# A masked scan for the log decays, and another order of 32x32 products, in a hybrid state-space and DeltaNet layer on Trainium2

## The chip, the cores and the metric

The kernel runs on one core of one Trainium2 chip. The metric is the device time of one execution in microseconds (us), as the median of several runs. A core has five engines that run side by side, each through its own list of instructions in order: TensorE (PE in the profile, with its weight loads as PEld), VectorE (DVE), ScalarE (ACT), GpSimd (POOL) and SyncE (SP), which here issues nearly all DMA transfers. They wait for each other by semaphores.

## The reference

One layer over a sequence of 1024 frames with 2048 channels: an RMSNorm, one input projection, an S5 state-space branch and a gated DeltaNet branch, gates, an output projection and a final RMSNorm. The change is in the DeltaNet branch (8 heads of 128), of which this is the part that matters:

```python
beta = jax.nn.sigmoid(beta_logit)
g = -jnp.exp(_f32(a_log)) * jax.nn.softplus(a_logit + _f32(dt_bias))   # log decay, per frame and head
...
gc = jnp.cumsum(g, axis=-1)                                            # within a chunk
decay = jnp.exp(jnp.where(causal, gc[..., :, None] - gc[..., None, :], -jnp.inf))
kk = jnp.einsum("bhncd,bhnsd->bhncs", k, k)
a_mat = jnp.where(strict, beta[..., None] * kk * decay, 0.0)
sol = lax.linalg.triangular_solve(a_mat, rhs, left_side=True, lower=True, unit_diagonal=True)
...
qk = jnp.einsum("bhncd,bhnsd->bhncs", q, k) * decay
```

So each chunk needs the matrix exp(gc[t] - gc[s]) for s <= t, which is exp of the sum of g over the frames after s up to t, and the inverse of a unit triangular matrix.

## The kernel before, in words

The kernel goes over the sequence in two passes of 512 frames. In each pass the heads are worked on in four chunks of 128 frames. The bulk of the work is projections on TensorE: each fp32 weight is split into a high and a low part in the fp32r type (`whi` by ACT, `wlo` by DVE, in `w_prep`), and each product is three matmuls of 128x512 (high by high, high by low, low by high). In the profile these are `p<-X,whi`, `p<-X,wlo`, `p<-Y,whi` and so on; this text calls them large matmuls.

All other work is written as generators in lanes (`epi`, `io`, `chain`, `prep`, `tab`, `s5`, `out`, `x`). After each group of three large matmuls `pump` calls `step` for every lane, and a lane's next piece is put into the program at that place if a small model of the engines' clocks (`Clock`, with the costs in `COST`) says that what it waits for is done and that DVE is not too far ahead of PE. So the order of all engines' instructions is fixed when the program is written, by the model's costs. The model charges an fp32 matmul of at most 32 output rows 0.3 of max(n/600, 0.06) us, whatever part of the array it uses, and a scan on DVE 0.07 + 0.00128 n us.

The pieces that the change touches:

- `gates_prep`, once in each pass, computes `gt` (g of every frame, for 8 heads x 4 chunks), splits it into `gth` and `gtl`, and makes the sums that are needed per frame with three small matmuls against `causal`, `after_r` and `ones`.
- `d_prep(h)`, once for each head and pass (16 times), in the lane `prep`. It first makes the log decays: POOL multiplies one part of g (`gth` or `gtl`) for two chunks with the mask `causal` into `dhl`, and PE multiplies `after_r` (1 where the frame is later) with it, four matmuls of 256 columns into one PSUM bank `pD`. ACT takes the exponential into the tile `E`, and POOL masks it. Then come the products of keys and queries (`pA`), and the inverse: 16x16 diagonal blocks on POOL (through DRAM, `lu_d` and `tu_d`), then joined to 32, 64 and 128 on PE. `Tm` is the same memory as `E`.
- The join to 32 and 64 is four bursts of 32x32 products, with operands in the tile that the profile calls M. First burst: `pG` from `LU` and `Tm`, 16 products, for each diagonal part b of the array (rows and columns 32b to 32b+31) and each chunk c. Second: `pU`, 32 products, from `g3` and `U`. Third: `pG`, 8 products, on two parts (rows 0 or 64, columns 32 or 96). Fourth: `pU`, 16 products, on four parts (rows 32 and 96, two column parts each). Every product is fp32 and shows in the trace as two matmuls, each with its weight load. After each burst ACT or DVE takes the bank out of PSUM.
- `d_chain(h)` in the lane `chain` runs the recurrence over chunks with the results.

A profile row has the line of the helper that records operations (L135) for nearly all work; tiles tell the groups apart. M is the one big block in which `E`, `LU`, `U`, `mi` and the heads' operands lie.

Of the kernel before, what the change touches and what calls it, by code (L numbers as in the profile page):

```python
# [11 lines left out]
F32 = mybir.dt.float32  # L12
F32R = mybir.dt.float32r
I32 = mybir.dt.int32
AF = mybir.ActivationFunctionType
# [21 lines left out]
P = 128  # L37
# [110 lines left out]
def kernel(  # L148
# [27 lines left out]
    V = Timed(nc.vector, "V", clock)  # L176
    S = Timed(nc.scalar, "S", clock)
    G = Timed(nc.gpsimd, "G", clock)
    PE = Timed(nc.tensor, "PE", clock)
    SP = Timed(nc.sync, "Q", clock)  # L180
# [3 lines left out]
    cpool = ctx.enter_context(tc.tile_pool(name="cpool", bufs=1))  # L184
# [4 lines left out]
    dram = ctx.enter_context(tc.tile_pool(name="dram", bufs=1, space=bass.MemoryType.DRAM))  # L189
# [4 lines left out]
    def nm(s):  # L194
        uid[0] += 1
        return f"{s}_{uid[0]}"

    def bank(i):
        return psum.tile([P, 512], F32, tag=f"p{i}", name=nm(f"p{i}"))
# [7 lines left out]
    def small(tag, n, rows=P):  # L207
        if tag not in small_at:
            small_at[tag] = small_at.get("", 0)
            small_at[""] = small_at[tag] + n  # L210
        return smalls[0:rows, small_at[tag]:small_at[tag] + n]

    def tt(o, a, b, op, eng=None):
        (eng or V).tensor_tensor(o, a, b, op=op)
# [10 lines left out]
    MUL, ADD, SUB, MAX, MIN = ALU.mult, ALU.add, ALU.subtract, ALU.max, ALU.min  # L225


    ident = cpool.tile([P, P], F32, name="ident")
    make_identity(nc, ident)
    ones = cpool.tile([P, P], F32, name="ones")  # L230
    G.memset(ones, 1.0)
    causal = cpool.tile([P, P], F32, name="causal")
# [3 lines left out]
    after = tmp[:, 0:P]  # L236
# [5 lines left out]
    for b in range(4):  # L242
# [2 lines left out]
        G.memset(off16[s32, 0, :], -1.0)  # L245
        G.affine_select(off16[s32, 0, :], off16[s32, 0, :], pattern=[[0, 16]], compare_op=ALU.is_ge,
                        fill=0.0, base=-16, channel_multiplier=1)
    after_r = cpool.tile([P, P], F32R, name="after_r")
    S.activation(after_r, after, AF.Copy)
    halfpi = cpool.tile([P, 1], F32, name="halfpi")  # L250
    G.memset(halfpi, float(np.float32(math.pi / 2)))

# [23 lines left out]

    lu_d = [dram.tile([4, 129, P], F32, name=f"lu_d{i}") for i in range(2)]
    tu_d = [[dram.tile([4, 129, P], F32, name=f"tu_d{i}{j}") for j in range(2)] for i in range(2)]
    nq_d = [dram.tile([1, P, 16], F32, name=f"nq_d{i}") for i in range(2)]
    st_d = dram.tile([8, P, P], F32, name="st_d")  # L280
    td_d = dram.tile([16, P, T], F32, name="td_d")
# [2 lines left out]
    def part(d, off, *dims):  # L284

        a = d[:, :, :] if len(d.shape) == 3 else d[:, :, :, :]
        return bass.AP(tensor=a.tensor, offset=a.offset + off, ap=[list(x) for x in dims])
# [46 lines left out]
    def exp_pool(o, v, n):  # L334
        G.tensor_tensor(o, pexp["e"][:, 0:1].broadcast_to([P, n]), v, op=ALU.pow)

    def gts(o, a, s1, s2, op0, op1):
        G.tensor_scalar(o, a, s1, s2, op0=op0, op1=op1)
# [10 lines left out]
    for ps_ in range(NPASS):  # L349
# [8 lines left out]
        for c in range(8):  # L358
            if c % 2 == 0 and 8 - u0 + c // 2 < 8:
                i = 8 - u0 + c // 2  # L360
# [503 lines left out]
    def hold(cond):  # L864
        while not cond():
            yield -1
# [147 lines left out]


    gt = cpool.tile([P, 8, 4], F32, name="gt")
    gth = cpool.tile([P, 8, 4], F32, name="gth")
    gtl = cpool.tile([P, 8, 4], F32, name="gtl")
    bt = cpool.tile([P, 8, 4], F32, name="bt")
    ex = cpool.tile([P, 3, 32], F32, name="ex")  # L1020
    negc = cpool.tile([P, 32], F32, name="negc")
# [1 line left out]
    def gates_prep(lg, ps_):  # L1023

        yield from hold(lambda: (ps_, "M0") in done)
        yield max(clock.wr[c] for c in clock.cells(lg))
        p2 = bank(5)
        fold = small("fold", 16, 32)
        tt(fold, ident[0:32, 0:16], ident[0:32, 16:32], ADD)
        for t in range(4):  # L1030
            PE.matmul(p2[:, t * 16:(t + 1) * 16], lhsT=lg[:, t * P:(t + 1) * P], rhs=fold, start=True, stop=True)
        l3 = p2[:, 0:64].rearrange("p (t h) -> p h t", h=16)
        mif = dw["mi"].rearrange("p c n -> p (c n)")
        av = mif[:, 0:32]
        a3 = av.rearrange("p (h t) -> p h t", h=8)
        S.activation(bt, l3[:, 0:8, :], AF.Tanh, scale=0.5)
        tt(a3, l3[:, 8:16, :], dtb.unsqueeze(2).broadcast_to([P, 8, 4]), ADD)
        gts(bt, bt, 0.5, 0.5, MUL, ADD)
        if ps_ == 0:
            exp_pool(nega, nega, 8)  # L1040
            gts(nega, nega, -1.0, 0.0, MUL, ADD)

        na, e1, w1, y0, e2, dl = (mif[:, (i + 1) * 32:(i + 2) * 32] for i in range(6))
        stt(na, av, -1.0, av, MUL, MIN)
        exp_pool(e1, na, 32)
        gts(w1, e1, 1.0, 1.0, MUL, ADD)
        S.activation(y0, w1, AF.Ln)
        yield
        gts(dl, w1, -1.0, 1.0, MUL, ADD)
        tt(dl, e1, dl, ADD, eng=G)  # L1050
        gts(na, y0, -1.0, 0.0, MUL, ADD)
        exp_pool(e2, na, 32)
        tt(dl, dl, e2, MUL, eng=G)
        tt(e2, w1, e2, MUL, eng=G)
        gts(e2, e2, 1.0, -1.0, MUL, ADD)
        tt(y0, e2, y0, ADD, eng=G)
        tt(y0, y0, dl, ADD, eng=G)
        gts(av, av, 0.0, 3e38, MAX, MIN)
        tt(y0, y0, av, ADD, eng=G)
        tt(gt, y0.rearrange("p (h t) -> p h t", h=8), nega.unsqueeze(2).broadcast_to([P, 8, 4]), MUL, eng=G)  # L1060
        yield
        gf = gt.rearrange("p h t -> p (h t)")
        S.activation(gth.bitcast(F32R), gt, AF.Copy)
        tt(gtl, gt, gth, SUB, eng=G)
        p3 = bank(5)
        for i, m in enumerate((causal, after_r.bitcast(F32), ones)):
            PE.matmul(p3[:, i * 32:(i + 1) * 32], lhsT=m, rhs=gf, start=True, stop=True)
        exf = ex.rearrange("p a n -> p (a n)")
        ts(exf, p3[:, 0:96], -1000.0, None, MAX)
        exp_pool(exf, exf, 96)  # L1070
        gts(negc, ex[:, 0, :], -1.0, 0.0, MUL, ADD)
        yield -1

    dhl = cpool.tile([P, 2, P], F32R, name="dhl")
    nk = [small(f"nk{i}", 4) for i in range(2)]
    nq = [small(f"nq{i}", 4) for i in range(2)]
    cc = [small(f"cc{i}", 4) for i in range(2)]
# [13 lines left out]
    def d_prep(h, ps_):  # L1091
        st = dw["set"][h % 2]
        kq, v, qk, U, kd = st["kq"], st["v"], st["qk"], st["U"], st["kd"]
        E, LU, mi = dw["E"], dw["LU"], dw["mi"]
        nk_, nq_, cc_ = nk[h % 2], nq[h % 2], cc[h % 2]
        qs_ = small(f"qs{h % 2}", 16)
        lud, tud = lu_d[h % 2], tu_d[h % 2]
        pD = bank(5)
        for j in range(2):
            for i, gg in enumerate((gth, gtl)):  # L1100
                tt(dhl, gg[:, h, 2 * j:2 * j + 2].unsqueeze(2).broadcast_to([P, 2, P]),
                   causal[:, None, :].broadcast_to([P, 2, P]), MUL, eng=G)
                yield
                PE.matmul(pD[:, j * 256:(j + 1) * 256], lhsT=after_r, rhs=dhl.rearrange("p c n -> p (c n)"),
                          start=(i == 0), stop=(i == 1))
        S.activation(E.rearrange("p c n -> p (c n)"), pD, AF.Exp)
        tt(E, E, hb4(causal), MUL, eng=G)
        yield -1
        yield from until((ps_, "q", h))
# [21 lines left out]
        for hf in range(2):  # L1131
            pA = bank((5, 2)[hf])
            for c in (2 * hf, 2 * hf + 1):
                PE.matmul(pA[:, (c % 2) * 256:(c % 2) * 256 + 256], lhsT=kq[:, c, 0, :],
                          rhs=kq[:, c].rearrange("p a n -> p (a n)"), start=True, stop=True)
# [10 lines left out]
        SP.dma_start(rows(lud), LU)  # L1146
        yield
        mif = mi.rearrange("p c n -> p (c n)")
        Ef = E.rearrange("p c n -> p (c n)")
        ba = mif[0:32, 0:256].rearrange("p (i m) -> p i m", i=16)  # L1150
        btm = mif[0:32, 256:512].rearrange("p (i m) -> p i m", i=16)
        bx = Ef[0:32, 0:256].rearrange("p (i m) -> p i m", i=16)
# [6 lines left out]
        for j in range(15):  # L1159
            n = 15 - j  # L1160
            a = ba[:, j, j + 1:16].unsqueeze(2).broadcast_to([32, n, j + 1])
            b = btm[:, j:j + 1, 0:j + 1].broadcast_to([32, n, j + 1])
# [22 lines left out]
        gs = mi  # L1185
        g3 = mi[:, :, 0:32]
        B4 = [slice(32 * b, 32 * b + 32) for b in range(4)]
        for b in B4:
            for c in range(4):
                PE.matmul(pG[b, c * 32:(c + 1) * 32], lhsT=LU[b, c, b], rhs=Tm[b, c, b], start=True, stop=True)  # L1190
        tt(g3, pG[:, 0:P].rearrange("p (c n) -> p c n", c=4),
           off16.rearrange("p a c -> p (a c)")[:, None, :].broadcast_to([P, 4, 32]), MUL)
        tt(g3, g3, id32[:, None, :].broadcast_to([P, 4, 32]), ADD)
        yield
        pU = bank(2)
        for b in B4:
            for c in range(4):
                PE.matmul(pU[b, c * 32:(c + 1) * 32], lhsT=g3[b, c, :], rhs=U[b, c, b], start=True, stop=True)
                PE.matmul(pU[b, P + c * 32:P + (c + 1) * 32], lhsT=U[b, c, b], rhs=g3[b, c, :],
                          start=True, stop=True)  # L1200
        for b in B4:
# [4 lines left out]

        pG = bank(5)
        pg = pG.rearrange("p (c n) -> p c n", c=4)
        for o in (0, 64):
            for c in range(4):  # L1210
                PE.matmul(pg[o + 32:o + 64, c, 0:32], lhsT=LU[o:o + 32, c, o + 32:o + 64],
                          rhs=Tm[o:o + 32, c, o:o + 32], start=True, stop=True)
        for o in (0, 64):
# [1 line left out]
        yield  # L1215
        pU = bank(2)
        pu = pU.rearrange("p (c n) -> p c n", c=4)
        for o in (0, 64):
            for c in range(4):
                PE.matmul(pu[o:o + 32, c, 0:32], lhsT=gs[o + 32:o + 64, c, 0:32],  # L1220
                          rhs=U[o + 32:o + 64, c, o + 32:o + 64], start=True, stop=True)
                PE.matmul(pu[o + 32:o + 64, c, 0:32], lhsT=U[o + 32:o + 64, c, o + 32:o + 64],
                          rhs=gs[o + 32:o + 64, c, 0:32], start=True, stop=True)
        for o in (0, 64):
# [9 lines left out]
        for c in range(4):  # L1234
            PE.matmul(pg[64:128, c, 0:64], lhsT=LU[0:64, c, 64:128], rhs=Tm[0:64, c, 0:64],
                      start=True, stop=True)
# [4 lines left out]
        for c in range(4):  # L1241
            PE.matmul(pu[0:64, c, 0:64], lhsT=gs[64:128, c, 0:64], rhs=U[64:128, c, 64:128],
                      start=True, stop=True)
# [448 lines left out]
```

## Time and profile before

| | before |
|---|---|
| median of 3 runs | 2998.33 us (2996.68 to 3001.13) |
| the profiled execution's own time | 3000.75 us |
| its span, first to last instruction | 2998.7 us |
| granted TensorE clock | 0.996 of full speed |
| PE busy | 2952.0 us (98%) in 15902 matmuls |
| DVE busy | 1676.4 us (56%) |
| ACT busy | 1149.5 us (38%) |
| POOL busy | 460.2 us (15%) |
| DMA, mean | 135 GB/s |

A group of instructions has the form: line, engine, operation, output tile <- input tiles, shape, count | busy time, mean ns of one | idle time of the engine just before them, and what ended it. In the order of time a row has its start, its duration, and how many like instructions it merges. A stretch of time (a window) shows how long an engine was busy in it and, behind x, how many of its instructions overlap the stretch. Matmuls are pipelined, so their durations overlap; the step from one start to the next is what one of them takes of PE's time.

### The profile page before, as it was taken

To read this page: it belongs to the slowest core of one execution; us is meant where nothing else is said; L and a number is where in the kernel's file an instruction comes from. 1 tells how busy PE (TensorE), PEld (TensorE's weight loads), DVE (VectorE), ACT (ScalarE), POOL (GpSimd) and SP (SyncE) were. 2 spreads that over 40 slices of the span, in tenths; PEclk is the share of its full clock that TensorE was granted. 3 is DMA by queue.
4 is the path that set the end of the run, shared out by engine and by line. 5 is a ranking of instruction groups with operands and counts; after the bars stand their busy time and mean duration, and the time that the engine had idled before them with its cause. 6 is when DMAs were issued, how large, how long until landed. Compare 5 with 4: busy or idle time off the path is not lost.

```text
span 2998.7 us, 42470 instructions
## 1 busy us (share of the span) xinstructions
PE 2952.0 (98%) x15902; PEld 2372.9 (79%) x15902; DVE 1676.4 (56%) x3130; ACT 1149.5 (38%) x2483; POOL 460.2 (15%) x857
## 2 busy tenths in 40 slices
PE   8999999999999999999999999999999999999998
PEld 6877777777777888888878777777777788888887
DVE  5746777777767422553454676567556633226542
ACT  5434544554544222334333344333433322223331
POOL 4413222122200000000024221222122000000000
PEclk9999999999999999999999999999999999999999
DMA  6435445444545644446354444544444464445541
GB/s 166 125 79 145 115 131 135 112 123 122 135 136 161 195 119 119 145 137 239 120 162 133 116 116 117 137 120 115 123 127 122 137 198 123 118 125 155 195 149 57
DMA packets 618240, 405.29 MB, mean 135 GB/s; under 512 B 91257, under 2 KB 551218, under 8 KB 616114
## 3 DMA queue, kind: packets, MB, share of 16 engines
q1 hardware_dynamic: 615730, 394.19, 46.2%
q0 software_dynamic: 2304, 8.39, 0.8%
q8 instruction: 125, 2.05, 0.3%
q14 instruction: 81, 0.66, 0.1%
HBM read 335.79 MB, written 66.72 MB: 134 GB/s over the span
## 4 chain that ended last, share of the span: by engine, by line
PE 85%; DVE 6%; ACT 3%; POOL 2%; DMA 2%; issue 2%; SPq 1%; DVEq 0%; POOLq 0%; ACTq 0%
PE p L135 85%; DVE G0a L135 2%; DVE M L135 2%; POOL M L135 2%; DVE wlo L135 1%; ACT M L135 1%; DVE tmp L135 1%; SPq L135 1%; POOL smalls L135 1%; DMA M<-tu_d 0%; ACT tmp L135 0%; ACT whi L135 0%; ACT L135 0%; ACT G0b L135 0%; DMA raw<-in_w_in_dram 0%
## 5 line engine op out<-in xcount | busy, mean ns | idle before, releaser
L135 PE MATMUL p<-X,whi 128*128 128x512 f32 (+1 forms) x4432 | 1396.4, 397 | 1.5 <-DVE whi L135 0.8
L135 DVE TENSOR_TENSOR wlo<-raw,whi 128x512 fp32r<-128x512 f32 x920 | 633.2, 700 | 744.2 <-ACT whi L135 743.5
L135 PEld LDWEIGHTS p<-X,whi 128*128 128x128 f32 (+1 forms) x4432 | 802.0, 188 | 175.3 <-issue 17.9
L135 PE MATMUL p<-X,wlo 128*128 128x512 f32 (+1 forms) x2184 | 852.7, 390 | 0.3 <-DVE wlo L135 0.2
L135 ACT ACTIVATE whi<-raw 128x512 fp32r<-128x512 f32 x917 | 557.8, 625 | 519.0 <-PE p L135 487.2
L135 PE MATMUL p<-Y,whi 128*128 128x512 f32 (+1 forms) x1808 | 568.0, 396 | 0.9 <-ACT p L135 0.9
L135 PEld LDWEIGHTS p<-X,wlo 128*128 128x128 f32 x2184 | 410.9, 188 | 89.1 <-DVE wlo L135 0.9
L135 PEld LDWEIGHTS p<-Y,whi 128*128 128x128 f32 (+1 forms) x1808 | 330.7, 187 | 71.3 <-issue 3.9
L135 PE MATMUL p<-Y,wlo 128*128 128x512 f32 x896 | 349.7, 390 | 0.0
L135 POOL TENSOR_SCALAR smalls<-smalls 128x4 f32<-128x4 f32 (+1 forms) x58 | 18.2, 313 | 1584.8 <-DVE smalls L135 1116.3
L135 ACT ACTIVATE tmp<-p 128x512 f32<-128x512 f32 x160 | 95.5, 597 | 400.9 <-PE p L135 393.6
L135 POOL TENSOR_TENSOR M<-M 32x28 f32<-32x28 f32 (+8 forms) x492 | 196.7, 400 | 282.8 <-DMA M<-lu_d 200.1
L135 DVE TENSOR_TENSOR G0a<-G0a 128x256 f32<-128x256 f32 (+1 forms) x432 | 211.1, 525 | 7.2 <-ACT G0a L135 3.5
L135 PEld LDWEIGHTS p<-M 32*32 32x32 f32 (+2 forms) x3072 | 153.0, 123 | 72.6 <-ACT M L135 28.8
L135 PEld LDWEIGHTS p<-Y,wlo 128*128 128x128 f32 x896 | 168.1, 188 | 36.5 <-DVE wlo L135 0.4
L135 PE MATMUL p<-M 32*32 32x32 f32 (+3 forms) x3072 | 186.9, 215 | 6.9 <-DMA M<-tu_d 3.8
L135 ACT ACTIVATE M<-p 32x128 f32<-32x128 f32 (+3 forms) x337 | 98.9, 297 | 161.1 <-PE p L135 157.5
L135 DVE SCALAR_TENSOR_TENSOR tmp<-tmp,vec 128x512 f32<-128x512 f32 x144 | 112.0, 778 | 11.7 <-ACT tmp L135 8.3
L135 DVE TENSOR_TENSOR G0a<-p,G0a 128x512 f32<-128x512 f32 x128 | 82.0, 681 | 13.9 <-PE p L135 13.8
L135 DVE TENSOR_TENSOR_SCAN G0a<-rho,scar,G0a 128x256 f32<-128x256 f32 x128 | 89.3, 738 | 0.0
L135 PE MATMUL p<-whi,G0a 128*128 128x512 f32 x280 | 88.5, 391 | 0.0
L135 PE MATMUL p<-whi,X 128*128 128x512 f32 x256 | 82.2, 393 | 0.0
(209 smaller groups left out, 2640.7 us busy)
## 6 DMA issues: line engine op xcount, KB each, us to landing
raw<-in_w_in_dram SPq DMA_DIRECT2D x324, 512.0 KB, 4.0
raw<-in_w_out_dram SPq DMA_DIRECT2D x56, 512.0 KB, 4.0
raw<-in_dn_w_up_dram SPq DMA_DIRECT2D x32, 512.0 KB, 4.1
raw<-in_s_w_up_dram SPq DMA_DIRECT2D x32, 512.0 KB, 3.9
td_d<-tmp SPq DMA_DIRECT2D x32, 256.0 KB, 2.0
M<-tu_d SPq DMA_DIRECT2D x32, 256.0 KB, 3.2
cs_d<-G0a SPq DMA_DIRECT2D x32, 256.0 KB, 2.2
yg_d<-G0a SPq DMA_DIRECT2D x64, 128.0 KB, 2.4
```

The lines of the kernel that those rows point to most:

```text
L135: return f(*a, **k)
```

## The change

The log decays come from a scan. `gates_prep` also transposes g on PE to one row per head and chunk (`grow`, 32 x 128) and stores it in DRAM (`g_d`). `d_prep` loads the head's four rows into `E` on all 128 partitions, and DVE scans each chunk with state = (g + state) * strict, where strict is 1 for frames later than the partition's own. After the scan the value is the sum of g over the frames after s up to t. The exponential and the mask are as before. `gth`, `gtl`, `dhl` and their matmuls go, and `afterk` stands in for `after_r` with the same content.

In the four bursts the loop over chunks becomes the outer one and the loop over parts the inner one; in the second and the fourth the two kinds of product are also taken apart, so that a kind is done for all parts before the other begins (in the fourth, within a chunk).

```diff
-    after_r = cpool.tile([P, P], F32R, name="after_r")
-    S.activation(after_r, after, AF.Copy)
+    afterk = cpool.tile([P, P], F32, name="afterk")
+    S.activation(afterk, after, AF.Copy)
+    strict = cpool.tile([P, P], F32, name="strict")
+    tt(strict, causal, ident, SUB, eng=G)
...
+    g_d = dram.tile([1, 32, P], F32, name="g_d")
...
         gf = gt.rearrange("p h t -> p (h t)")
-        S.activation(gth.bitcast(F32R), gt, AF.Copy)
-        tt(gtl, gt, gth, SUB, eng=G)
         p3 = bank(5)
-        for i, m in enumerate((causal, after_r.bitcast(F32), ones)):
+        PE.transpose(p3[0:32, 96:96 + P], gf, ident)
+        for i, m in enumerate((causal, afterk, ones)):
             PE.matmul(p3[:, i * 32:(i + 1) * 32], lhsT=m, rhs=gf, start=True, stop=True)
+        grow = mif[0:32, 256:256 + P]
+        S.activation(grow, p3[0:32, 96:96 + P], AF.Copy)
+        SP.dma_start(g_d[0], grow)
...
-        pD = bank(5)
-        for j in range(2):
-            for i, gg in enumerate((gth, gtl)):
-                tt(dhl, gg[:, h, 2 * j:2 * j + 2].unsqueeze(2).broadcast_to([P, 2, P]),
-                   causal[:, None, :].broadcast_to([P, 2, P]), MUL, eng=G)
-                yield
-                PE.matmul(pD[:, j * 256:(j + 1) * 256], lhsT=after_r, rhs=dhl.rearrange("p c n -> p (c n)"),
-                          start=(i == 0), stop=(i == 1))
-        S.activation(E.rearrange("p c n -> p (c n)"), pD, AF.Exp)
+        Ef = E.rearrange("p c n -> p (c n)")
+        SP.dma_start(Ef, part(g_d, h * 512, (0, P), (1, 512)))
+        yield
+
+        for c in range(4):
+            V.tensor_tensor_scan(E[:, c, :], E[:, c, :], strict, 0.0, op0=ADD, op1=MUL)
+        S.activation(Ef, Ef, AF.Exp)
         tt(E, E, hb4(causal), MUL, eng=G)
...
-        for b in B4:
-            for c in range(4):
+        for c in range(4):
+            for b in B4:
                 PE.matmul(pG[b, c * 32:(c + 1) * 32], lhsT=LU[b, c, b], rhs=Tm[b, c, b], start=True, stop=True)
...
-        for b in B4:
-            for c in range(4):
+        for c in range(4):
+            for b in B4:
                 PE.matmul(pU[b, c * 32:(c + 1) * 32], lhsT=g3[b, c, :], rhs=U[b, c, b], start=True, stop=True)
+        for c in range(4):
+            for b in B4:
                 PE.matmul(pU[b, P + c * 32:P + (c + 1) * 32], lhsT=U[b, c, b], rhs=g3[b, c, :],
                           start=True, stop=True)
...
-        for o in (0, 64):
-            for c in range(4):
+        for c in range(4):
+            for o in (0, 64):
                 PE.matmul(pg[o + 32:o + 64, c, 0:32], lhsT=LU[o:o + 32, c, o + 32:o + 64],
                           rhs=Tm[o:o + 32, c, o:o + 32], start=True, stop=True)
...
-        for o in (0, 64):
-            for c in range(4):
+        for c in range(4):
+            for o in (0, 64):
                 PE.matmul(pu[o:o + 32, c, 0:32], lhsT=gs[o + 32:o + 64, c, 0:32],
                           rhs=U[o + 32:o + 64, c, o + 32:o + 64], start=True, stop=True)
+            for o in (0, 64):
                 PE.matmul(pu[o + 32:o + 64, c, 0:32], lhsT=U[o + 32:o + 64, c, o + 32:o + 64],
                           rhs=gs[o + 32:o + 64, c, 0:32], start=True, stop=True)
```

Three places show how the program's order changes. The first is PE at the start of `d_prep` for the last head of the second pass, before the change; X and Y are the large matmuls' operands, `ident,M` is the transpose in the chain of the head before.

```order
L135 MATMUL p_2443_19235<-dhl,after_r 128x256
L135 MATMUL p_2440_19207<-Y_1453_11621,whi_19130 128x512 x2
L135 MATMUL p_2440_19207<-Y_1453_11621,wlo_19131 128x512
L135 MATMUL p_2440_19207<-X_1454_11622,whi_19169 128x512 x2
L135 MATMUL p_2440_19207<-X_1454_11622,wlo_19170 128x512
L135 MATMUL p_2443_19235<-dhl,after_r 128x256
L135 MATMUL p_2440_19207<-X_1454_11622,whi_19169 128x512 x2
L135 MATMUL p_2440_19207<-X_1454_11622,wlo_19170 128x512
L135 MATMUL p_2449_19277<-ident,M_1692_13095 128x128 x4
```

And after the change, around the same transpose:

```order
L135 MATMUL p_2437_19247<-X_1446_11591,whi_19228 128x512 x2
L135 MATMUL p_2437_19247<-X_1446_11591,wlo_19229 128x512
L135 MATMUL p_2445_19311<-ident,M_1684_13064 128x128 x4
L135 MATMUL p_2437_19247<-X_1446_11591,whi_19228 128x512 x2
L135 MATMUL p_2437_19247<-X_1446_11591,wlo_19229 128x512
```

The matmuls with `dhl` are gone from between the large matmuls, and nothing stands in their place on PE.

The second place is DVE at the start of that head's `d_prep`, after the change. M with `strict` are the scans (printed as a scalar-tensor-tensor form), `wlo` the weight splits, `tmp` the convolution, G0a the S5 branch.

```order
L135 SCALAR_TENSOR_TENSOR tmp<-tmp,vec 128x512 x3
L135 TENSOR_TENSOR X_1828_14211<-M_1684_13064,X_1828_14211 128x512
L135 SCALAR_TENSOR_TENSOR M_1684_13064<-M_1684_13064,strict 128x128 x4
L135 TENSOR_TENSOR wlo_19192<-raw_19050,whi_19191 128x512
L135 TENSOR_TENSOR wlo_19209<-raw_19050,whi_19208 128x512
L135 SCALAR_TENSOR_TENSOR G0a_12911<-rho,scar,G0a_12911 128x256 x2
```

The four scans stand in DVE's list ahead of two weight splits; before the change DVE had no work for the log decays.

The third place is SP there, after the change: `M<-g_d` is the load of the head's rows, `raw` the weights.

```order
L135 DMA G0a_12911<-w_d 128x256
L135 DMA raw_19117<-in_w_in_dram 128x8x128
L135 DMA M_1684_13064<-g_d 128x512
L135 DMA raw_19189<-in_w_in_dram 128x8x128
L135 DMA raw_19226<-in_w_in_dram 128x8x128
```

The load stands between two weight loads, where before there were weight loads alone.

More of the change, by code (lines that the diff above doesn't have):

```diff
@@ L1016 @@
     gt = cpool.tile([P, 8, 4], F32, name="gt")
-    gth = cpool.tile([P, 8, 4], F32, name="gth")
-    gtl = cpool.tile([P, 8, 4], F32, name="gtl")
     bt = cpool.tile([P, 8, 4], F32, name="bt")
@@ L1072, in gates_prep @@
         yield -1
-    dhl = cpool.tile([P, 2, P], F32R, name="dhl")
     nk = [small(f"nk{i}", 4) for i in range(2)]
@@ L1148, in d_prep @@
         mif = mi.rearrange("p c n -> p (c n)")
-        Ef = E.rearrange("p c n -> p (c n)")
         ba = mif[0:32, 0:256].rearrange("p (i m) -> p i m", i=16)
```

## The prediction

> **What bounds the kernel now.** I read the page's first part and its chain of waits first.
>
> ```profile
> span 2998.7 us, 42470 instructions
> PE 2952.0 (98%) x15902; PEld 2372.9 (79%) x15902; DVE 1676.4 (56%) x3130; ACT 1149.5 (38%) x2483; POOL 460.2 (15%) x857
> PE 85%; DVE 6%; ACT 3%; POOL 2%; DMA 2%; issue 2%; SPq 1%; DVEq 0%; POOLq 0%; ACTq 0%
> ```
>
> TensorE (PE) is busy for 98% of the span and holds 85% of the chain that ended last. So time taken off PE comes off the end nearly in full, and work on DVE, ACT or POOL costs only where PE then waits for it. Next I read the groups of instructions, with each shape apart, for what the change touches.
>
> ```profile
> L135 PE MATMUL p<-M 32*32 32x32 f32 x2304 | 64.1, 193 | 4.1 <-DMA M<-tu_d 3.8 <-ACT M L135 0.2
> L135 PE MATMUL p<-dhl,after_r 128*128 128x256 f32 x64 | 20.6, 322 | 1.6 <-POOL dhl L135 1.6
> L135 PEld LDWEIGHTS p<-dhl,after_r 128*128 128x128 f32 x64 | 12.1, 188 | 7.8 <-POOL dhl L135 6.2
> L135 DVE TENSOR_TENSOR_SCAN G0a<-rho,scar,G0a 128x256 f32<-128x256 f32 x128 | 89.3, 738 | 0.0
> ```
>
> The 2304 small products are 144 for each of 16 heads (8 in each of two passes over the sequence): every fp32 product shows as two matmuls, so the four bursts of a head have 32, 64, 16 and 32. Busy times are unions of overlapping durations and don't give a price. For that I read the order of time on PE, in a head of the second pass (start, duration, what, count).
>
> ```profile
> 1908.90 0.39 PE L135 MATMUL p<-Y,wlo 128*128 128x512 f32 x1
> 1909.22 0.89 PE L135 MATMUL p<-M 32*32 32x32 f32 x32
> 1910.04 0.73 PE L135 MATMUL p<-Y,whi 128*128 128x512 f32 x2
> ...
> 1911.62 1.91 PE L135 MATMUL p<-M 32*32 32x32 f32 x64
> 1913.46 0.73 PE L135 MATMUL p<-Y,whi 128*128 128x512 f32 x2
> ...
> 1915.72 0.59 PE L135 MATMUL p<-M 32*32 32x32 f32 x16
> 1916.24 0.73 PE L135 MATMUL p<-Y,whi 128*128 128x512 f32 x2
> ...
> 1917.83 0.60 PE L135 MATMUL p<-M 32*32 32x32 f32 x32
> 1918.36 0.73 PE L135 MATMUL p<-X,whi 128*128 128x512 f32 x2
> ```
>
> A burst ends with a fixed gap. The second one covers 1911.62 to 1913.53, its last matmul lasts about 0.19 (mean 193 ns), so that one started at 1913.34, and the next large matmul starts at 1913.46: 0.12 later. The same 0.12 taken from each burst leaves 0.70, 1.72, 0.40 and 0.41 us in which matmuls are started: 22, 27, 25 and 13 ns for each. The fourth burst is twice as fast as the others, and it alone already changes between two parts of the array.
>
> How many run at once tells why. The same head, PE alone, work on M alone, in stretches of 0.01 us; x is the number of matmuls in flight.
>
> ```profile
> core 0: us, PE busy (x), PEclk, DMA share, GB/s
> 1912.00:1912.01 0.01, 0.01 (x6) 1.00 0.68 205
> 1918.00:1918.01 0.01, 0.01 (x13) 1.00 0.00 0
> 1918.07:1918.08 0.01, 0.01 (x19) 1.00 0.00 0
> 1918.15:1918.16 0.01, 0.01 (x18) 1.00 0.00 0
> ```
>
> At 1912.00, inside one diagonal part's run, 6 are in flight: 193/6 = 32 ns from one to the next. At 1918.00 the fourth burst has its first two parts going (13), and from 1918.07 the last products of those and the first of the next two run together: 18 or 19, that is 193/18.5 = 10 ns. So one part takes a matmul every 32 ns, and parts run beside each other, four of them at once here.
>
> **The change, part by part.** (1) Order of the products. In the first and second burst neighbours now go round four diagonal parts; in the third they alternate between two parts; in the fourth they go round four. At 10 ns with four parts and 193/13 = 15 ns with two, a head's bursts need 32 x 10 = 0.32, 64 x 10 = 0.64, 16 x 15 = 0.24 and 32 x 10 = 0.32 us, 1.52 in place of 0.70 + 1.72 + 0.40 + 0.41 = 3.23. That is 1.71 us a head, **27 us** for 16. Bounds: four parts at 32 ns each would give 8 ns, 0.26 + 0.51 + 0.24 + 0.26 = 1.27, a gain of 31 us; if everything only reached the fourth burst's present average of 13 ns, 0.42 + 0.83 + 0.24 + 0.41 = 1.90, 21 us. I take the 10 ns because it is measured with four parts at work. The gap of 0.12 at each end stays. PE's place in the order does not move for it: the planner's clock charges these products alike in any order. The ACT copies and DVE products that follow a burst start at its end, and so does the large work that covers them, so that distance stays.
>
> A rule speaks against this. The Trainium skill, "TensorEngine Tiling (Array Packing)", section "Gotcha 1: PSUM Pressure", says that different row parts can't access the same PSUM bank at one time, and here all four parts write one bank. Taken at its word, no two row parts would overlap; the trace disagrees, since the 19 in flight at 1918.07 belong to two row parts that write one bank. What it would do to the time is rival C.
>
> (2) The 64 matmuls of 256 columns that made the log decays go. Two of them, with their neighbours:
>
> ```profile
> 1946.69 0.39 PE L135 MATMUL p<-Y,wlo 128*128 128x512 f32 x1
> 1947.48 0.39 PE L135 MATMUL p<-dhl,after_r 128*128 128x256 f32 x1 [0.40 <-POOL dhl L135]
> 1947.70 0.63 PE L135 MATMUL p<-Y,whi 128*128 128x512 f32 x2
> ...
> 1951.15 0.28 PE L135 MATMUL p<-dhl,after_r 128*128 128x256 f32 x1
> 1951.26 0.63 PE L135 MATMUL p<-X,whi 128*128 128x512 f32 x2
> 1951.73 0.39 PE L135 MATMUL p<-X,wlo 128*128 128x512 f32 x1
> 1951.95 0.62 PE L135 MATMUL p<-X,whi 128*128 128x512 f32 x2
> ```
>
> A large matmul takes 0.23 to the next one (1951.26 to 1951.73 is two). The one at 1951.15 costs 0.11; the one at 1947.48 costs 1.01 - 0.23 = 0.78, as PE waited for POOL. Undisturbed, 64 x 0.12 = 7.7 us; the upper bound is the group's whole 20.6 us. Add the waits named for them (1.6 on the matmuls, and of the 6.2 on the weight loads about a third that isn't covered by the matmul before): **11 us**.
>
> (3) Added on PE: a transpose in each of two passes, two matmuls each. Beside the three small products there (next fence) it is about 0.3 us a time: 0.6 us lost in all, at most 1.
>
> (4) Added on DVE: four scans over 128 columns per head, 64 in all. The nearest row is the scan over 256 columns, 738 ns; half of it is 0.37, and with a fixed part I take 0.4: 1.6 us a head, 26 us on DVE. Queued behind them in order are the products that split the weights (wlo), on which PE feeds, and the state updates of the chain of heads. The planner charges a scan 0.23, so DVE runs 0.7 us behind its plan at that place.
>
> ```profile
> L135 PE MATMUL p<-ident,M 128*128 128x128 f32 x256 | 41.7, 286 | 9.0 <-DVE M L135 9.0
> L135 PE MATMUL p<-state,M 128*128 128x128 f32 x256 | 39.8, 278 | 4.9 <-DVE state L135 4.9
> L135 PE MATMUL p<-gt,causal 128*128 128x32 f32 x4 | 0.7, 259 | 1.0 <-POOL gt L135 1.0
> 2100.00:2200.00 100.00, 63.16 (x120) 1.00 0.46 121
> M<-tu_d SPq DMA_DIRECT2D x32, 256.0 KB, 3.2
> SPq L135 <- DVE wlo L135: 983.0, 337, 14.4
> ```
>
> DVE is busy for 63% of a hundred microseconds in that stage, so the extra 1.6 in about 100 fits, and the weight splits run ahead: they are made four chunks early, each chunk being 12 large matmuls, 4 x 12 x 0.23 = 11 us. PE now loses 9.0 + 4.9 = 14 us waiting for DVE in the chain of heads over the whole run. I take 2 us more from the scans. Bounds: 0, and 26 if every scan were in PE's way.
>
> (5) Added on the queue of SP: a 256 KB load per head and two small stores. The nearest transfer, M from tu_d, has the same size and lands in 3.2 us; PE waited 3.8 us in all for 32 of those (first group above). For 16 loads of which PE waits only through DVE I take 1 us, bounds 0 and 4. Behind the load on SP stand the weight loads, which wait for DVE anyway (last row). (6) Off PE and free: on POOL the 64 products for the removed matmuls go, on ACT a small copy; the 128x512 exponential reads SBUF in place of PSUM. POOL is busy 15%, ACT 38%; these cover themselves, and would be worth nothing even uncovered.
>
> Sum: -27 - 11 + 0.6 + 2 + 1 = **-34 us**. Against the profiled execution's own 3000.75 that is 2967; that execution was 2.4 above the median of the three, so against the median of 2998.33 I forecast **2964**.
>
> **Rivals.** A, the forecast: 2954 to 2973.
>
> B, the queue feeds too slowly. Once the first 32 matmuls of the long burst are gone, new ones might arrive no faster than its present 27 ns: 0.32 + 32 x 0.027 = 1.18 for it, 0.54 gained there, 0.38 + 0.16 + 0.09 in the others, 19 us in all in place of 27, so 34 - 8 = 26 us, 2972 (2976 with the low price of part 2). For it: no row shows more than 32 fast ones in succession. Against: nothing in the second burst stalls at its end.
>
> C, one part at a time, which ends slower. If going round made the parts take turns, 144 x 32 ns = 4.6 us a head against 3.23: 22 us lost, with the other terms 22 - 11 + 3.6 = +15, 3013. It decides from about 26 ns a matmul, where the loss eats the 8 us of the removed work. Against it: 18 in flight at 1918.15. The rule quoted above would end here.
>
> D, the scans and their load stand in PE's way: a head would pay landing and scans, 3.2 + 1.6 = 4.8 us, 77 us for 16, slower from 2.3 us a head on. Half of it gives 3000. For it: SP and DVE work in order. Against: tu_d's loads, 3.8 us for 32.
>
> E, a floor for starts. If the third burst's present 25 ns were a floor between any two starts, the four bursts would need 144 x 25 = 3.6 us, 6 us lost in all, 6 - 11 + 3.6 = -1, 2997. Against it: 13 ns over the 32 of the fourth burst. The Trainium skill, "TensorE: Matmul & The Clock Gate", section "Wait — 56ns, not 53.3ns?", states such a floor of about 25 ns from start to start; the trace disagrees, with 10 ns.
>
> F, more than forecast: the parts reach their own 8 ns, and the removed matmuls were worth 15, midway to their bound: -31 - 15 + 1 = -45, 2953, with nothing lost to DVE.
>
> **How the numbers follow.** Chances: A 0.63, F 0.10, B 0.14, C 0.04, D 0.05, E 0.04. The likeliest gives 2964. The range 2950 to 2980 holds F's time, A and B and leaves C, D and E out. A measurement of this kernel can tell about 0.2% (6 us) from no change. Faster than that: A, F, B and the milder part of D, 0.90. The same: E and a share of D, 0.05. Slower: C and the rest of D, 0.05.
>
> **What would show it.** In the profile after, the rows of the second burst should read about 0.64 + 0.12 = 0.76 us to the next large matmul and not 1.84, the first 0.44 and not 0.82, and in the bursts' middle about 18 in flight. Rows with dhl are gone, and a scan over 128 columns stands with 64 of about 400 ns. The waits of PE for DVE M and DVE state stay within a few us of 14. The forecast is wrong if the second burst stays above 1.2 us (B, C, E), if 0.12 gaps appear inside a burst, or if PE's idle time for wlo, state or raw grows by over 10 us (D).

## The result, and the profile after

| | before | after |
|---|---|---|
| median of 4 runs each, on one chip | 2999.38 us (2996.68 to 3001.13) | 2961.76 us (2960.76 to 2966.81) |
| ratio, 95% interval | | 0.9879 [0.9862, 0.9896] |
| the profiled execution's span | 2998.7 us | 2959.6 us |
| granted TensorE clock | 0.996 | 0.996 |

Faster by 1.2%, 37.6 us between the medians, where 34 were forecast (2964); the median before has one run more here than in the table ahead of the prediction. The page of the changed kernel begins like this; the third line is its chain of waits.

```profile
span 2959.6 us, 42410 instructions
PE 2908.3 (98%) x15840; PEld 2335.3 (79%) x15840; DVE 1681.5 (57%) x3194; ACT 1151.8 (39%) x2487; POOL 410.2 (14%) x792
PE 85%; DVE 5%; POOL 4%; DMA 3%; issue 2%; ACT 2%; SPq 1%; DVEq 0%; POOLq 0%; ACTq 0%
```

PE still holds 85% of the chain: what came off the end came off PE. The four bursts of a head of the second pass, in order of time on PE (start, duration, what, count):

```profile
2268.06 0.45 PE L135 MATMUL p<-M 32*32 32x32 f32 x32
2268.45 0.73 PE L135 MATMUL p<-X,whi 128*128 128x512 f32 x2
...
2270.03 0.75 PE L135 MATMUL p<-M 32*32 32x32 f32 x64
2270.71 0.73 PE L135 MATMUL p<-Y,whi 128*128 128x512 f32 x2
...
2272.97 0.43 PE L135 MATMUL p<-M 32*32 32x32 f32 x15
2274.52 0.21 PE L135 MATMUL p<-M 32*32 32x32 f32 x1 [1.11 <-issue]
...
2276.26 0.45 PE L135 MATMUL p<-M 32*32 32x32 f32 x32
2276.65 0.72 PE L135 MATMUL p<-Y,whi 128*128 128x512 f32 x2
```

The second burst goes from its start to the next large matmul in 0.68 us, where it took 1.84. With 0.19 for its last matmul, the starts cover 0.56 us, 8.8 ns each; in the first and the fourth burst they cover 0.26, 8.2 ns each. The third needs 0.25 in 14 of the 16 heads; here its last matmul came 1.11 us late, in another head 1.40, and nothing in the trace says what ended that.

How much each group takes of PE is found by adding, over all PE instructions, the step from one start to the next less the idle time in it. What was idle is added by what ended it. The time before PE's first matmul, 5.3 and 5.7 us, is in the row of all other work.

| us of PE, whole span | before | after | forecast for the difference |
|---|---|---|---|
| 32x32 products (2304) | 59.6 | 29.6 | -27 |
| matmuls with dhl (64), and waits for POOL dhl | 10.4 + 1.6 | 0 | -11 |
| transposes of g | 0 | 0.2 | +0.6 |
| idle, ended by DVE wlo | 0.3 | 13.1 | (scans: +2 on DVE in all) |
| idle, ended by DVE M and DVE state | 14.3 | 6.6 | |
| idle, ended by DVE Y and DVE G0a | 4.0 | 0.3 | |
| idle, all else (without POOL dhl) | 12.5 | 16.6 | (load: +1) |
| all other work | 2896.0 | 2893.2 | 0 |
| sum | 2998.7 | 2959.6 | -34 |

The small products and the removed matmuls came out about as forecast. The idle time hides a surprise in a sum that hardly moved (32.7 before, 36.6 after). The view of PE's waits has for the kernel before (total, times, longest):

```profile
PE p L135 <- DVE M L135: 9.2, 6, 5.2
PE p L135 <- DVE state L135: 4.9, 4, 2.5
PE p L135 <- DVE wlo L135: 0.2, 1, 0.2
```

and for the changed one:

```profile
PE p L135 <- DVE wlo L135: 13.0, 3, 10.6
PE p L135 <- DVE M L135: 5.9, 5, 3.9
PE p L135 <- DVE state L135: 0.4, 1, 0.4
```

One wait of 10.6 us is new. In order of time, DVE and then PE around it, after the change:

```profile
208.76 0.69 DVE L135 TENSOR_TENSOR wlo<-raw,whi 128x512 fp32r<-128x512 f32 x1 [12.00 <-ACT whi L135]
209.37 4.29 DVE L135 SCALAR_TENSOR_TENSOR G0b<-ident,G0b 128x128 f32<-128x128 f32 x16
213.57 14.73 DVE L135 TENSOR_TENSOR Y<-Y 128x1024 f32<-128x1024 f32 x12
228.21 0.75 DVE L135 SCALAR_TENSOR_TENSOR M<-p,vec,M 128x512 f32<-128x512 f32 x1
228.88 1.28 DVE L135 TENSOR_TENSOR wlo<-raw,whi 128x512 fp32r<-128x512 f32 x2
...
218.37 0.61 PE L135 MATMUL p<-X,whi 128*128 128x512 f32 x2
229.61 0.80 PE L135 MATMUL p<-X,wlo 128*128 128x512 f32 x1 [10.62 <-DVE wlo L135]
```

Before, the same twelve products stood on DVE in four pieces, the first and the last of them these:

```profile
215.36 3.61 DVE L135 TENSOR_TENSOR Y<-Y 128x1024 f32<-128x1024 f32 x3
...
231.79 3.68 DVE L135 TENSOR_TENSOR Y<-Y 128x1024 f32<-128x1024 f32 x3
```

They belong to the one-time setup of the S5 branch, a job in the lane `s5` that `step` takes up only while DVE is less than SETUP = 2.0 us ahead of PE by the model. What is left when the S5 work needs it is drained: written into the program in one piece. With twelve in one piece, and 4.3 us of other products straight ahead of them, DVE makes no weight split from 209.46 to 228.88 us, which is 19.4 us. PE lives on its stock of splits until 218.98, 9.5 us, and then waits. Before the change the longest stretch without a split round one of the four pieces was 5.9 us.

The scans themselves, by their group:

```profile
L135 DVE TENSOR_TENSOR_SCAN M<-M,strict x64: 393/400/426, 92.9 to 2213.0; 128x128 f32<-128x128 f32 x64
```

64 of them at 400 ns in the middle (least, median and most), as estimated.

### The profile page after: what moved, and what is told of

It is laid out like the page before. It is cut to its first block, busy times and chain, and to the rows that moved or that the text cites. A ratio compares the mean times of both kernels' runs of the same rounds, so it can differ in the third digit from the quotient of the medians.

```text
span 2959.6 us, 42410 instructions
## 1 busy us (share of the span) xinstructions
PE 2908.3 (98%) x15840; PEld 2335.3 (79%) x15840; DVE 1681.5 (57%) x3194; ACT 1151.8 (39%) x2487; POOL 410.2 (14%) x792
## 3 DMA queue, kind: packets, MB, share of 16 engines
q0 software_dynamic: 2304, 8.39, 0.8%
## 4 chain that ended last, share of the span: by engine, by line
PE 85%; DVE 5%; POOL 4%; DMA 3%; issue 2%; ACT 2%; SPq 1%; DVEq 0%; POOLq 0%; ACTq 0%
PE p L135 85%; POOL M L135 3%; DVE M L135 1%; DVE G0a L135 1%; DVE wlo L135 1%; DVE Y L135 1%; DMA M<-tu_d 1%; SPq L135 1%; DMA lu_d<-M 1%; ACT M L135 1%; POOL ex L135 1%; DVE tmp L135 0%; DMA M<-lu_d 0%; ACT whi L135 0%; DMA tu_d<-M 0%
## 5 line engine op out<-in xcount | busy, mean ns | idle before, releaser
L135 PEld LDWEIGHTS p<-M 32*32 32x32 f32 (+2 forms) x3072 | 123.1, 122 | 74.9 <-ACT M L135 27.9
L135 PE MATMUL p<-M 32*32 32x32 f32 (+3 forms) x3072 | 157.2, 216 | 9.0 <-DMA M<-tu_d 3.9
L135 ACT ACTIVATE M<-p 32x128 f32<-32x128 f32 (+3 forms) x323 | 89.9, 281 | 113.8 <-PE p L135 110.4
L135 ACT ACTIVATE M<-M 128x128 f32<-128x128 f32 (+2 forms) x98 | 40.2, 412 | 119.5 <-DVE M L135 106.7
```

The lines of the kernel that those rows point to most:

```text
L135: return f(*a, **k)
```

## The experiments

Each time stands beside runs of the kernel before on the same chip. Where one execution is named, no interval can be given.

**e1: the order of products alone.** The kernel before, with the loops of the four bursts turned round as in the change, and the log decays still made by matmuls.

```diff
-        for b in B4:
-            for c in range(4):
+        for c in range(4):
+            for b in B4:
                 PE.matmul(pG[b, c * 32:(c + 1) * 32], lhsT=LU[b, c, b], rhs=Tm[b, c, b], start=True, stop=True)
...
```

> The kernel before with the new order of the 32x32 products alone; the log decays stay as they were. Theory (the gain is PE's time in the bursts, and it comes off the end in full): the bursts fall from 59.6 us in all to about 29.6 us as in the changed kernel, the removed matmuls stay with 10.4 us, so the kernel before minus 30 us: about 2969. Rival (the bursts' gain is partly eaten by the copies out of PSUM that follow each burst, since PE reaches the next burst sooner): PE's idle time for ACT M and DVE M grows, and less than 22 us is left, above 2977.

Measured: 2971.89 us (2971.10 to 2973.81), ratio 0.9910 [0.9895, 0.9925]. By the accounting above the small products fell by 30.4 us and PE's idle time rose by 5.1. The rival expected that in the waits for ACT M and DVE M, which hardly moved (12.1 us before, 11.9 here). Of the 5.1, 3.6 are one wait for wlo, at the same S5 setup: here DVE made its products in a piece of three and one of nine:

```profile
217.75 3.60 DVE L135 TENSOR_TENSOR Y<-Y 128x1024 f32<-128x1024 f32 x3
224.29 10.91 DVE L135 TENSOR_TENSOR Y<-Y 128x1024 f32<-128x1024 f32 x9
```

So the order of the products alone is worth 27 us, and it moves the plan: PE's list differs from that of the kernel before from the first head's third burst on. The reason is read from the code and not tried by itself: the model keeps a time for each 32 partitions of a tile. With b outermost the first part of a bank was written early, and its copy could be planned early; with c outermost all four parts are written at the end.

**e2: the scan alone.** The changed kernel with the loops of the four bursts as they were.

```diff
-        for c in range(4):
-            for b in B4:
+        for b in B4:
+            for c in range(4):
                 PE.matmul(pG[b, c * 32:(c + 1) * 32], lhsT=LU[b, c, b], rhs=Tm[b, c, b], start=True, stop=True)
...
```

> The changed kernel with the old order of the 32x32 products: the scan alone. Theory 1 (the 12 products of 128x1024 of the S5 setup stand in one piece on DVE because the scan moved the planner's clocks): PE again waits some 10 us for wlo near 220 us of the span, so of the 10.4 us of removed matmuls and some 8 us of smaller waits about 6 us is left: about 2993. Theory 2 (that piece comes from the shorter bursts): no such wait, about 2982. In both, the scans have about 400 ns and nobody waits for the load of the decays by more than 1 us.

Measured: 2993.14 us (2991.35 to 2996.55), ratio 0.9980 [0.9971, 0.9989]. The matmuls with dhl are gone (-10.4), and the wait is there:

```profile
232.10 0.80 PE L135 MATMUL p<-X,wlo 128*128 128x512 f32 x1 [10.62 <-DVE wlo L135]
```

The scan takes 12 us off PE (the matmuls and their waits for POOL) and brings a plan that loses 10.6 at one place; 6 are left. The parts of the change, 27 and 6 us, add up to 33 of the 38.

**e3: a wider limit for the setup.** The changed kernel; only the gate of the S5 setup lets more through.

```diff
-SETUP = 2.0
+SETUP = 4.0
```

> The changed kernel with one planner constant, the lag of DVE behind PE at which the S5 setup may still issue work, at 4.0 in place of 2.0; in DVE's list the 12 products of the S5 setup then stand in three pieces with weight splits between them. Theory (the 10.6 us wait of PE for wlo comes from their standing in one piece of 14.7 us, longer than the 11 us by which splits run ahead): the wait goes and the time falls by about 10 us, to about 2951. Rival (DVE has too much work in that stretch, wherever it stands): PE's waits move to other weight splits or to the chain of heads there and the time stays within 3 us of 2962.

Measured: 2948.45 us (2946.85 to 2951.39), ratio 0.9831 [0.9818, 0.9845]: 13.3 us less than the change in the profiled spans. The twelve products stand in three pieces, the last of them at 224.26, and what is left of PE's waits for wlo is 2.3 us:

```profile
208.66 7.26 DVE L135 TENSOR_TENSOR Y<-Y 128x1024 f32<-128x1024 f32 x6
219.67 3.61 DVE L135 TENSOR_TENSOR Y<-Y 128x1024 f32<-128x1024 f32 x3
224.26 3.61 DVE L135 TENSOR_TENSOR Y<-Y 128x1024 f32<-128x1024 f32 x3
```

The longest stretch without a weight split round one of the pieces is now 7.6 us, where e1 had 11.4 and a wait of 3.6, and the changed kernel 19.4 and a wait of 10.6. That the 10.6 us came from the piece of twelve is shown. This version beats both kernels, and it is the base of the experiments e6 to e9.

**e4: eight parts of the array in place of four.** In the second burst the products of the second kind go to the next column part and to a bank of their own, and take turns with the first kind, so that neighbours go round eight parts.

```diff
+        pT = bank(4)
         for c in range(4):
             for b in B4:
                 PE.matmul(pU[b, c * 32:(c + 1) * 32], lhsT=g3[b, c, :], rhs=U[b, c, b], start=True, stop=True)
-        for c in range(4):
-            for b in B4:
-                PE.matmul(pU[b, P + c * 32:P + (c + 1) * 32], lhsT=U[b, c, b], rhs=g3[b, c, :],
+            for i, b in enumerate(B4):
+                PE.matmul(pT[B4[(i + 1) % 4], c * 32:(c + 1) * 32], lhsT=U[b, c, b], rhs=g3[b, c, :],
                           start=True, stop=True)
```

> The changed kernel, but in the second burst the second kind of product goes to other column parts of the array, into a bank of its own, and alternates with the first kind after every four products, so that eight parts of the array are at work; the copies read it from there, so the result is the same. Theory 1 (each part takes one matmul in 32 ns, nothing else limits): the 64 matmuls, which take 0.56 us with four parts, take about 0.30. Theory 2 (the queue feeds matmuls at about 8 to 9 ns): they stay at 0.55 to 0.60 us.

Measured: 2966.59 us in one execution, 5 us more than the changed kernel's median; 3.7 us of that is idle time. The burst takes what it took, but not in the same way. Its row, and the matmuls in flight (behind x) in stretches of 0.01 us:

```profile
2275.63 0.75 PE L135 MATMUL p<-M 32*32 32x32 f32 x64
...
2275.78:2275.79 0.01, 0.01 (x31) 1.00 0.29 102
...
2276.00:2276.01 0.01, 0.01 (x11) 1.00 0.34 102
2276.10:2276.11 0.01, 0.01 (x21) 1.00 1.49 512
```

The first 32 matmuls start within 162 ns, 5.2 ns each, and 31 are in flight 0.15 us after the burst's start. Then nothing starts for 76 ns, and the rest come in twos every 16.6 ns, 8.3 ns each. This reads as if 32 matmuls, with their 32 weight loads, stood ready when the burst began, and as if what comes behind them is fed at 8.3 ns. The changed kernel bears it out: with four parts the first 32 matmuls of its second burst start within 262 ns, and behind them its starts come in twos too, about 16.6 ns apart. Four parts give 8.2 ns, so the two limits lie close together. What feeds the matmuls no run looked into. The Trainium skill, "TensorE: Matmul & The Clock Gate", Part 3, section "The mechanism", gives TensorE a window of 64 instructions; the 32 and 32 here agree. The Trainium skill, "TensorE: Matmul & The Clock Gate", Part 3, section "Measured speedup vs the span model", counts about 4 ns for each further part of the array; here it was 5.2.

**e5: two parts in place of four.** The second burst goes round two diagonal parts, then round the other two.

```diff
-        for c in range(4):
-            for b in B4:
-                PE.matmul(pU[b, c * 32:(c + 1) * 32], lhsT=g3[b, c, :], rhs=U[b, c, b], start=True, stop=True)
...
+        for pair in (B4[0:2], B4[2:4]):
+            for c in range(4):
+                for b in pair:
+                    PE.matmul(pU[b, c * 32:(c + 1) * 32], lhsT=g3[b, c, :], rhs=U[b, c, b], start=True, stop=True)
...
```

> The changed kernel, but in the second burst the products go round two diagonal parts of the array (first parts 0 and 1 for all chunks and both kinds, then 2 and 3) in place of four. Theory (a part takes one matmul in 32 ns, so two parts give 16 ns, until the 8.3 ns at which the queue is refilled binds): the 64 matmuls take about 64 x 16 = 1.0 us in place of 0.56, and PE's time in the four bursts of all heads grows from 29.6 to about 37 us. Rival (the gain came from leaving the same part at all, and two are as good as four): it stays at 0.6 us.

Measured: 2973.83 us in one execution, with 3000.28 for the kernel before.

```profile
2283.53 1.11 PE L135 MATMUL p<-M 32*32 32x32 f32 x64
2284.56 0.73 PE L135 MATMUL p<-Y,whi 128*128 128x512 f32 x2
```

The starts cover 1.11 - 0.19 = 0.92 us, 14 ns each, where four parts need 0.56 and one part 1.72 in the order before. A part takes a matmul each 32 ns, and two parts give one each 16, less the overlap where the pairs change. All bursts together rose from 29.6 to 35.6 us. The rest of the 12.5 us in the span is 3.0 us of idle time (DMA M<-tu_d +4.5, others less) and slower large matmuls (+3.7).

**e6: every scan twice, and the planner not told.** On e3. The copy goes to LU, which is written over later, and the model charges nothing for it, so that PE's list stays row for row the same.

```diff
         for c in range(4):
+            nc.vector.tensor_tensor_scan(LU[:, c, :], E[:, c, :], strict, 0.0, op0=ADD, op1=MUL)
             V.tensor_tensor_scan(E[:, c, :], E[:, c, :], strict, 0.0, op0=ADD, op1=MUL)
```

> The kernel of the run with the planner constant at 4.0, with each scan of the log decays done twice, the first time into a tile that is written anew later; the planner is not told, so the order of all other work stays. 64 scans of 0.4 us are added, 26 us on DVE. Theory (the scans lie beside PE's work): at most 3 us more than 2948, below 2952. Rival (DVE's list is on PE's path in the heads, the added scans hold the weight splits and the state updates): 8 us or more, 2956 to 2974.

Measured: 2979.05 us (2977.64 to 2986.90), ratio 0.9939 [0.9926, 0.9951]. That is 30.6 us above e3, for 64 x 0.42 = 27 us of added DVE work. My theory, that DVE's work for the scans lies beside PE's, expected almost nothing and fell; the rival's side is right, and even its upper end of 2974 is passed. PE's waits in this kernel:

```profile
PE p L135 <- DVE M L135: 8.6, 5, 3.7
PE p L135 <- DVE state L135: 8.1, 5, 3.3
PE p L135 <- DVE G0a L135: 7.8, 5, 1.6
PE p L135 <- ACT M L135: 7.6, 7, 1.8
...
1865.51 1.08 PE L135 MATMUL p<-G0a,G0b 128*64 128x256 f32 x6 [1.55 <-DVE G0a L135]
```

The wait for G0a, which e3 has not at all, comes in five heads at 1.55 to 1.57 us each, and four added scans are 1.68. These places in PE's list had no slack. In all PE's idle time is 20.6 us longer than in e3. The other 9 us are work that takes longer (large matmuls +5.9); the granted clock was 0.994 where e3 had 0.997. This was no chance of one execution: the five of e6 had 0.991 to 0.995, the four of e3 0.996 to 0.998. What lowered it the runs don't show.

**e7: the planner charges a scan its true cost.** On e3; 0.07 + 0.0026 x 128 is 0.40 us.

```diff
-"tensor_tensor_scan": {"V": (0.07, 1.28e-3)},
+"tensor_tensor_scan": {"V": (0.07, 2.6e-3)},
```

> The kernel of the run with the planner constant at 4.0, with the planner's cost of a scan set to what the trace shows (0.07 us and 2.6 ns a column in place of 1.28 ns), for the scans of the S5 branch too. Theory (PE's waits for DVE state, DVE M and ACT G0b come from the planner thinking DVE earlier than it is): they fall from about 11 us to half, and the time by 3 to 5 us, to about 2944. Rival (those waits have other causes, and a planner that sees DVE later holds the S5 branch back): no change or slower, 2946 to 2960.

Measured: 2947.93 us (2945.24 to 2958.53), ratio 0.9834 [0.9815, 0.9852], no difference from e3, so the theory's 3 to 5 us did not come and the rival's range holds. The waits only move: PE waits 8.3 us for DVE M (5.9 in e3), 2.3 for DVE state (4.4), 3.2 for ACT G0b (0.2). The 0.17 us that the model misses on a scan, 0.7 a head, cost nothing that shows.

**e8: every scan twice, and the planner told.** On e7, so that both scans are charged 0.40.

```diff
         for c in range(4):
+            V.tensor_tensor_scan(LU[:, c, :], E[:, c, :], strict, 0.0, op0=ADD, op1=MUL)
             V.tensor_tensor_scan(E[:, c, :], E[:, c, :], strict, 0.0, op0=ADD, op1=MUL)
```

> The changed kernel with the setup limit 4.0, each scan doubled once more as before, but now the planner knows of both scans and charges each 0.07 + 0.0026 n us (0.40 us for 128 columns). The added scan writes into LU, which is written over afterwards; nothing of the result changes. Theory L (what cost 30.6 us with the doubling that the planner did not know was lateness against the plan: a wait placed too early in PE's list): told of it, the planner puts the later PE work further down, and the 27 us of added DVE work costs at most a quarter, so 2949 to 2955, with PE's waits for DVE M, DVE state and DVE G0a together under 18 us. Rival V (DVE's volume in a head is on the path of the chain, whatever the plan): again 15 us or more, 2963 or above, with those waits over 22 us as in the doubling not told (24.5).

Measured: 2951.35 us (2950.25 to 2952.17), with 3001.74 for the kernel before: ratio 0.9833 [0.9818, 0.9848], where e7 had 0.9834. The 27 us of DVE work that cost 30.6 in e6 cost nothing here. The expectation of theory L holds for PE's waits too:

```profile
PE p L135 <- DVE M L135: 12.9, 6, 5.2
...
PE p L135 <- DVE state L135: 1.6, 2, 1.1
```

14.5 us together, and no wait for G0a. So DVE's added volume need not be on PE's path. What e6 paid for is lateness against a list made without that work. But e8 has another list as a whole (PE's idle time is 5.1 us longer than in e7, for DVE M and DVE Y above all, and its other work 3.2 shorter), and how much of the difference a new list brings by luck the two runs don't separate.

**e9: no scans.** On e3. The exponential is taken of the loaded g itself, so the decays are missing from what the kernel computes, and only its time is read.

```diff
-        for c in range(4):
-            V.tensor_tensor_scan(E[:, c, :], E[:, c, :], strict, 0.0, op0=ADD, op1=MUL)
```

> The changed kernel with the setup limit 4.0 and no scans at all: the exponential is taken of the loaded g itself, so the decays are not those of the reference and only the time is of use. The load stays, and the planner knows that the scans are gone. It takes 64 x 0.40 = 26 us off DVE. Theory L (planned scans lie beside PE's work): the time stays within 5 us of that with the scans, 2943 to 2950. Rival V (the volume on DVE is paid on PE): 15 us or more come off, 2933 or below, with PE's waits for DVE M and DVE state falling from 10.4 us to under 4.

Measured: 2971.94 us (2971.36 to 2975.00), ratio 0.9905 [0.9889, 0.9922]: with 26 us less on DVE the kernel is some 22 us *slower* than e3. Both expectations missed. PE's waits have the one for G0a again:

```profile
PE p L135 <- DMA M<-tu_d: 8.1, 5, 3.4
PE p L135 <- DVE M L135: 8.0, 6, 3.8
PE p L135 <- DVE G0a L135: 7.0, 6, 1.4
```

It comes at one place in six heads, up to 1.38 us each time. DVE and PE there, in order of time:

```profile
2044.66 0.69 DVE L135 TENSOR_TENSOR M<-p,ex 128x512 f32<-128x512 f32 x1 [1.73 <-ACT M L135]
2045.27 0.75 DVE L135 TENSOR_TENSOR G0a<-G0a 128x256 f32<-128x256 f32 x2
...
2046.16 1.08 PE L135 MATMUL p<-G0a,G0b 128*64 128x256 f32 x6 [1.34 <-DVE G0a L135]
```

DVE's list has a product that waits 1.73 us for ACT ahead of the G0a products, and PE's matmuls on G0a wait behind both. The heads of the second pass are planned alike, so one unlucky neighbour is paid in each. Idle time is 15.6 us longer than in e3 in all; of the 7.8 us of slower work 4.0 are large matmuls, with a granted clock of 0.995 where e3 had 0.997. What in the plan without scans makes this neighbour I have not traced. The run also limits what e8 shows: that planned DVE work *can* cost nothing, not that any plan will absorb it.

## Why the prediction was right, and where it was not

**(1) The products: the mechanism was right, its size off.** -27 forecast, -30.0 measured. The mis-sized term is "at 10 ns with four parts": 8.2 ns in the first and fourth burst, 8.8 in the second. The 10 came from stretches in which two parts were ending and two beginning; four parts at 32 ns each, the bound of 31 us, was nearly the truth. In the middle of the second burst the trace has

```profile
2270.24:2270.25 0.01, 0.01 (x26) 1.00 0.46 154
2270.50:2270.51 0.01, 0.01 (x23) 1.00 0.57 205
```

23 to 26 matmuls in flight and not about 18. The 0.12 us behind each burst stayed. That one part's pace is 32 ns and parts run beside each other is shown from both sides, by e5 (two parts, 0.92 us) and e4 (eight parts, 5.2 ns for the first 32).

"PE's place in the order does not move for it" was wrong: e1 has another list from the first head on, at a cost of 5.1 us of idle time. That the charges are alike doesn't make the plan alike, since the model also keeps the times at which pieces are written.

**(2) The matmuls with dhl: right.** -11 forecast, 10.4 and 1.6 of waits measured. The 0.12 us for an undisturbed one holds for half of the 64; the others took 0.20 to 0.22, which the forecast met with its share of the weight loads' waits. **(3)** +0.6 forecast, +0.2 measured.

**(4) The scans: the price was right, the plan that they brought was not foreseen, and the sum came out by cancelling.** A scan takes 400 ns. The cover of 11 us, "the weight splits run ahead", was nearly its size too: PE lived on it for 9.5 us. But it is a cover only for a DVE that comes back in time. At the S5 setup DVE stayed away for 19.4 us, and PE lost 10.6 there (e3 takes the piece apart, and the wait goes). Against that, PE's waits for DVE M, state, Y and G0a fell by 11.4 in the new plan. The sign "stay within a few us of 14" for DVE M and state was missed with 6.6. The "2 us more" stands beside +1.3 measured (+2.2 over all of PE's waits for DVE), but neither number is the scans' own cost: in e8, planned, added scans cost nothing, and in e6, not planned, 30.6 us for 27 of work. The charge of 0.23 in the model, from which the prediction worked out 0.7 us of delay, did not matter (e7).

**(5) The load: right in size.** DVE waited 0.2 us for it in all, and PE's wait for M<-tu_d went from 3.8 to 4.0. PE's idle time ended by G0b<-v_d, 2.5 us, is new in the profile after; the load alone does not bring it, as e3 has the same loads and not this wait. **(6)** POOL fell to 14%; nothing came of it at the end.

**The rivals.** B was half right: the pace changes behind the 32nd matmul, but to 8.3 ns and not 27, and it costs the second burst about 0.03 us. C and E fall by the row of the second burst: 8.8 ns a matmul, with four parts in one bank. The rule on PSUM banks quoted in the prediction did not hold for them, and the floor of 25 ns neither. D falls, as DVE hardly waits for the load. Yet its mark, "PE's idle time for wlo, state or raw grows by over 10 us", was met by wlo alone (+12.7), from another cause: a mark that names a wait doesn't name its cause. F's time, 2953, was not reached; its 8 ns were.

The range held, but the distance to its middle was luck by some 10 us: without the piece of twelve the kernel stands at 2948, below the range's lower end.

## What to carry to other kernels

In this kernel small fp32 products that share one diagonal part of the array follow each other at 32 ns; let neighbours use different parts, and four parts give 8 ns, about as much as eight gave in a burst of 64. Where a planner writes all engines' lists, an edit to one part can re-plan the rest: look in the trace after for one long wait at a place the edit doesn't touch, since here a single constant of the planner was worth 13 us beside the change's 38. Idle capacity on an engine is not free by itself: the same 27 us on a DVE busy for 57% cost 31 where the plan did not know of them and nothing in a plan that did, and 26 us less work cost 22 in another plan.

## What the runs showed of the hardware that was not expected

- In the burst of 64 small fp32 products the first 32 matmuls start 5.2 ns apart on eight parts; behind them come two per 16.6 ns (e4, and behind its 32nd the changed kernel too). More than four parts therefore gained nothing in a burst of 64.
- A wait in PE's third burst is ended by nothing that the profile has: in two heads of the changed kernel, 1.4 and 1.1 us, and in one of e4, 0.8 us, but in none of e1, e2 and e3. It stays open.
- The granted clock was 0.997 in e3 and 0.994 in e6, whose PE list is the same but with 20.6 us more idle time; the large matmuls took 5.9 us more with it. e1, with 0.997 and 43.1 us idle where e3 has 29.6, speaks against idle time alone as the cause, and e8, with the scans of e6 and 0.996, against the added work alone. It stays open.
